# A decoder layer on eight cores: sample caches loaded per head, transfers reordered, and norm squares added in pairs on GpSimd

## The chip, the cores and the metric

The kernel runs on the eight cores of one Trainium2 chip. All cores run the same program, each on its own prompt and on four of the 32 sample tokens. The metric is the device time in microseconds (us) of the slowest core. The cores form two dies, cores 0 to 3 and cores 4 to 7.

In some runs the cores of one die, or of both, are granted a lower TensorE clock, and the run is longer by several per cent; such a run is called slow here. Only fast runs are compared with fast runs, and cores of an undisturbed die with each other.

Short names used by the profile: PE is TensorE's matmuls, PEld its weight loads, DVE is VectorE, ACT is ScalarE, POOL is GpSimd, SP is SyncE.

## The reference

One layer, for 2048 prompt tokens and 4 sample tokens per core, width 1024:

```python
x += 0.5 * SwiGLU(RMSNorm(x))                 # FFN1, hidden width 2816
z  = RMSNorm(x) @ w_in                        # one projection for all branches
# A: dilated window attention, 3 groups x 4 heads x 128. A sample token reads
#    128 rows of its own k/v cache per head, and its new k and v
# B: HGRN2 recurrence, 4 heads, state 128x128
# C: attention into 256 memory tokens, 4 heads (a sample token: cached k/v)
x += merge_branches(A, B, C, gates(z)) @ w_o
x += 0.5 * SwiGLU(RMSNorm(x))                 # FFN2
y  = RMSNorm(x)                               # final norm
# also returned: the window caches shifted by one row (here called bulk copies,
# 44 MB a core, from DRAM to DRAM), the memory k/v, the HGRN states
```

## The kernel before

Activations lie transposed, the 1024 features on partitions in 8 chunks of 128. The 2052 token columns are cut into six tiles of 336 to 352 columns, three for each half of the tokens. The order of stages is: the norm at the start, FFN1, the mixer (branches A, B and C), merge and output projection of half 0 (`merge(0)`, `merge_out(0)`), the same for half 1, FFN2 with the final norm.

Every operation is recorded by a helper (so all have line L80 in the profile), and a list scheduler with a simple cost model fixes for each engine one static order in which it issues. In the trace of the kernel before (core 4) GpSimd keeps to that order: it idles 6.57 us for an x tile in front of three weight loads (`wgu`), until 31.18 us, and only then, at 32.73 us, issues the load of `w_mk`, which needs no x and has the seventh of the seven weight buffers free.

```python
def sq(k, c):                            # sum of squares of one chunk, for a norm
    n = FT[k][1]                         # columns of tile k
    b = P.tile(brp)                      # bf16 buffer
    actf(b.t[:, 0:n], xv(k, c), AF.Square, [dx[k][c]], [b.d])        # ScalarE
    if c == 0:
        pss[k] = P.tile(psS)
    p = pss[k]
    # the matmul with a matrix of 1/1024 sums over partitions: 8 for each norm of a tile
    mm(p.t[:, 0:n], ones_n, b.t[:, 0:n], c == 0, c == 7, [b.d, dc], [p.d])

def merge_out(half, done):
    bs = [load_w(w_o[q]..., 2048) for q in range(4)]
    for k in HT[half]:
        for dp in range(8):
            if half:                     # half 1: x comes back from DRAM chunk by chunk
                xr = P.tile(frp)
                P.dma(SP, ... out=xr.t[:, 0:n], in_=xd[k][:, dp * n:(dp + 1) * n] ...)
            # ... 8 matmuls, x = 0.5 * result + x on VectorE ...
            sq(k, dp)
        done(k)

def att_sample():                        # runs at the end of the mixer
    # ...
    for b in range(NS):                  # 4 sample tokens
        bk = load_w(csk[b]..., 1536)     # cached keys of 12 heads
        bv = load_w(csv[b]..., 1536)     # cached values
        # ... two more loads: cached memory keys and values ...
        # 20 one-column score matmuls, Exp on ScalarE, 20 one-column value
        # matmuls, one ones-matmul, a copy by ScalarE
        yield 1

# bulk copies: one every ~30 us through FFN1, mixer, merge and FFN2
P.dma(ACT, ..., pool="bulk", rel=210e3 + q * 1.45e6 / nbulk)

# the start
load_x(0, xt, 4)
# ...
P.dma(ACT, lambda e: e.dma_start(out=vec[:, 0:52], in_=vecs), writes=[dc])
for k in range(3):
    # ... load tile k, sq(k, c) for 8 chunks, then h = x * rstd * g
gate_up(0, wgu[0], hook)   # weights wait for x only from the second load on

# how the mixer's three branches are interleaved when they are recorded
for _ in spread([A(), HG(), chain(*(mem_att(ti) for ti in range(4)))], [210, 92, 22]):
    pass
```

In the profile `wp` are the weight buffers, `br` and `fr` small bf16 and f32 buffers, `cb` holds the ones-matrices, `ps`, `hb` and `nd` are PSUM banks, `XA` and `XB` hold x or, in the mixer, intermediate results, and `hT` is the normalised x.

The softmax here doesn't subtract the row's maximum and nothing guards it: scores larger than these inputs give would overflow.

## Time and profile before

| | before |
|---|---|
| time, three runs | 1920.39, 1923.39, 2134.98 us (the last is slow) |
| profiled run (fast), cores | 1903.4 to 1930.0 us, slowest core 4 |
| mean granted clock | 0.972 to 0.976 on all cores |

The page of the slowest core, its part 1 (busy us, share of the span, instructions) and part 4 (the chain of work that ended last, by engine):

```profile
PE 1783.9 (92%) x12080; PEld 1123.2 (58%) x12143; DVE 712.1 (37%) x1415; ACT 735.9 (38%) x1227; POOL 296.7 (15%) x437
...
PE 81%; DMA 8%; DVE 3%; issue 3%; ACT 2%; SPq 1%; POOL 1%; DVEq 0%; ACTq 0%; POOLq 0%
```

TensorE is the limit, and 8% of the chain is DMA. Where TensorE is not busy is seen by stage. These are windows of core 4; the columns are the window, its length, each engine's busy us with its instructions, the granted clock, the busy share of the DMA engines, and GB/s:

```profile
0.00:100.00 100.00, 66.17 (x381) 39.23 (x382) 26.27 (x60) 46.49 (x77) 10.69 (x26) 0.95 0.66 128
100.00:517.00 417.00, 416.93 (x2870) 279.96 (x2870) 106.75 (x212) 130.56 (x217) 37.33 (x71) 1.00 0.60 112
527.00:1060.00 533.00, 478.08 (x3108) 257.16 (x3166) 291.50 (x582) 294.70 (x480) 123.90 (x142) 0.97 0.62 135
1060.00:1120.00 60.00, 31.67 (x300) 17.66 (x301) 19.35 (x23) 22.54 (x35) 10.92 (x19) 0.72 0.95 183
1404.00:1453.00 49.00, 32.77 (x210) 20.08 (x210) 18.56 (x38) 15.61 (x28) 2.11 (x4) 0.90 0.84 167
1460.00:1900.00 440.00, 439.98 (x3033) 295.82 (x3031) 103.06 (x203) 107.59 (x185) 36.41 (x69) 1.00 0.55 100
```

FFN1 (100 to 517 us) and FFN2 (1460 to 1900) are full. The start loses 34 us, the mixer (527 to 1060) 55 (42 to 48 on the cores whose trace is complete: core 4's lacks 58 matmul records here, 3108 against 3166 weight loads), its end (1060 to 1120) 28 of 60 us at a clock of 0.72 and a DMA share of 0.95, and the second `merge_out` (1404 to 1453) 16 us on this core.

The timeline of PE on core 4 shows the waits themselves: start and duration in us, the instruction group, and in brackets the idle time before it with what ended it.

```profile
21.32 4.85 PE L80 MATMUL ps<-hT,wp 128*128 128x352 bf16 x16 [2.16 <-DVE hT L80]
...
54.95 0.72 PE L80 MATMUL ps<-hT,wp 128*128 128x336 bf16 x2 [8.75 <-DVE hT L80]
55.46 0.76 PE L80 MATMUL nd<-hT,wp 128*128 128x336 bf16 x2
56.02 0.76 PE L80 MATMUL ps<-hT,wp 128*128 128x336 bf16 x2
...
57.70 0.35 PE L80 MATMUL nd<-hT,wp 128*128 128x336 bf16 x1
...
58.18 0.45 PE L80 MATMUL nd<-hT,wp 128*128 128x336 bf16 x2
58.46 0.45 PE L80 MATMUL ps<-hT,wp 128*128 128x336 bf16 x2
...
1083.73 0.46 PE L80 MATMUL hb<-br,wp 128*128 128x1 bf16 x12 [4.44 <-ACT br L80]
...
1092.52 0.35 PE L80 MATMUL ps<-mqs,wp 128*128 128x1 bf16 x8 [4.96 <-DMA wp<-cmk]
1093.38 0.46 PE L80 MATMUL hb<-br,wp 128*128 128x1 bf16 x12 [0.52 <-ACT br L80]
1100.11 2.29 PE L80 MATMUL ps<-hT,wp 128*128 128x512 bf16 x5 [6.26 <-DMA wp<-w_mq]
...
1112.59 2.50 PE L80 MATMUL ps<-hT,wp 128*128 128x352 bf16 x8 [2.88 <-DMA wp<-w_gb]
```

The projections of FFN1 begin at 21.32 us, and the third x tile is ready only at 54.95. At the mixer's end the one-column matmuls (`128x1`) are the sample's: PE waits 4.44 us for their Exp on ScalarE, 4.96 us for a cached memory key (`cmk`), and then for the weights queued behind the caches (`w_mq`, `w_gb`).

One DMA issue of the first 60 us (KB, and us from issue to landing) shows that the queues are crowded at the start; `memt`, 1024 KB, is in flight then and takes 14.2 us:

```profile
vec<-vecs ACTq DMA_DIRECT2D x1, 26.0 KB, 10.5
```

`vecs`, 26 KB that the first norm needs, takes 10.5 us to land. And this is what PE waited for in the second `merge_out` of core 4 (us in total, times, longest):

```profile
PE hb L80 <- ACT br L80: 16.8, 9, 3.4
```

The ones-matmuls (`hb`) there wait for squares, which wait for x, which waits for the 24 chunk loads.

### The profile page before, as it was taken

The page shows a single profiled execution, that of the slowest core. Times are in us where ns is not written, and L with a number is a line of the kernel's source. Part 1 is how long each engine was busy: PE and PEld are TensorE (multiplying, and loading weights), DVE is VectorE, ACT ScalarE, POOL GpSimd, SP SyncE. Part 2 cuts the span into 40 slices and gives each one's busy share as a digit, 9 for nine tenths or more (in the row PEclk, how much of TensorE's full clock was granted, in tenths as well). Part 3 has the DMA queues.
Part 4 walks back from the last instruction along what each step waited for, and adds up shares of the span by engine and source line. Part 5 has one row for each costly group of instructions (what it writes and reads, how often), then busy time and mean ns, then how long its engine had stood idle before and what let it go on. Part 6 is the DMA issues. An engine that isn't in the chain of part 4 may idle for free.

```text
span 1930.0 us, 32870 instructions; the slowest of 8 cores (1903.4 to 1930.0 us)
## 1 busy us (share of the span) xinstructions
PE 1783.9 (92%) x12080; PEld 1123.2 (58%) x12143; DVE 712.1 (37%) x1415; ACT 735.9 (38%) x1227; POOL 296.7 (15%) x437
## 2 busy tenths in 40 slices
PE   4899999999998998889889489999979999999997
PEld 1566666666644544454445256666645666666665
DVE  2313323221332437675756333463342221332213
ACT  4435324221253646676725343353333221232212
POOL 1010000000131421314001222212200000100010
PEclk9999999999999999999989699999998999999999
DMA  9394449445799864545534986756784654584443
GB/s 190 66 202 74 72 115 159 82 74 109 138 188 167 207 135 100 122 99 124 129 99 111 192 142 110 129 102 96 127 176 89 121 107 81 128 177 76 60 67 104
DMA packets 92699, 233.96 MB, mean 121 GB/s; under 512 B 33280, under 2 KB 43776, under 8 KB 90112
## 3 DMA queue, kind: packets, MB, share of 16 engines
q0 software_dynamic: 40320, 125.98, 42.9%
q1 hardware_dynamic: 50400, 61.73, 10.3%
q10 hardware_dynamic: 1824, 44.15, 8.6%
q8 instruction: 101, 1.65, 0.4%
q14 instruction: 54, 0.44, 0.1%
HBM read 321.27 MB, written 80.51 MB: 208 GB/s over the span
## 4 chain that ended last, share of the span: by engine, by line
PE 81%; DMA 8%; DVE 3%; issue 3%; ACT 2%; SPq 1%; POOL 1%; DVEq 0%; ACTq 0%; POOLq 0%
PE ps L80 46%; PE nd L80 27%; PE hb L80 8%; DMA vd<-br 2%; DMA wp<-cmv 2%; DMA fr<-xd 2%; SPq L80 1%; ACT br L80 1%; DVE XB L80 1%; DMA wp<-w_mq 1%; DMA wp<-cmk 1%; DMA pv<-fr 1%; ACT fr L80 1%; DVE br L80 1%; DVE fr L80 1%
## 5 line engine op out<-in xcount | busy, mean ns | idle before, releaser
L80 PE MATMUL ps<-hT,wp 128*128 128x336 bf16 (+4 forms) x4198 | 699.7, 313 | 31.0 <-DVE hT L80 14.3
L80 PEld LDWEIGHTS ps<-hT,wp 128*128 128x128 bf16 x4232 | 394.2, 98 | 263.7 <-issue 39.5
L80 PE MATMUL nd<-hT,wp 128*128 128x336 bf16 (+2 forms) x2160 | 352.6, 310 | 0.0
L80 ACT ACTIVATE fr<-ps,vec 128x336 f32<-128x336 f32 (+3 forms) x270 | 150.5, 558 | 341.7 <-PE ps L80 339.2
L80 PEld LDWEIGHTS nd<-hT,wp 128*128 128x128 bf16 x2160 | 211.7, 98 | 103.1
L80 PE MATMUL ps<-actb,wp 128*128 128x336 bf16 (+2 forms) x1620 | 260.2, 309 | 0.0
L80 PEld LDWEIGHTS ps<-actb,wp 128*128 128x128 bf16 x1620 | 158.4, 98 | 76.7
L80 ACT ACTIVATE fr<-nd,vec 128x352 f32<-128x352 f32 (+3 forms) x181 | 101.0, 558 | 233.4 <-PE nd L80 233.0
L80 DVE TENSOR_TENSOR actb<-ps,fr 128x336 bf16<-128x336 f32 (+2 forms) x159 | 81.5, 514 | 283.2 <-PE ps L80 244.4
L80 PE MATMUL nd<-actb,wp 128*128 128x336 bf16 (+2 forms) x1068 | 173.3, 308 | 0.0
L80 PEld LDWEIGHTS nd<-actb,wp 128*128 128x128 bf16 x1068 | 104.2, 98 | 50.5
L80 POOL TENSOR_TENSOR fr<-fr 128x512 f32<-128x512 f32 (+3 forms) x96 | 104.2, 1092 | 175.4 <-DVE fr L80 145.9
L80 POOL DMA_DIRECT2D wp<-wgu x88 | 46.7, 530 | 506.4 <-PE ps L80 268.7
L80 DVE TENSOR_TENSOR actb<-nd,fr 128x336 bf16<-128x336 f32 (+2 forms) x105 | 53.8, 513 | 183.3 <-PE nd L80 168.6
L80 ACT ACTIVATE br<-XB,vec 128x352 bf16<-128x352 f32 (+3 forms) x104 | 56.3, 569 | 164.1 <-DVE XB L80 161.7
L80 PE MATMUL hb<-hT,wp 128*128 128x512 bf16 (+1 forms) x543 | 111.4, 342 | 2.8 <-DMA wp<-w_hqf 1.2
L80 ACT ACTIVATE br<-XA,vec 128x336 bf16<-128x336 f32 (+1 forms) x96 | 52.2, 574 | 141.9 <-DVE XA L80 141.6
L80 PE MATMUL hb<-br,cb 128*128 128x336 bf16 (+3 forms) x199 | 60.7, 322 | 39.0 <-ACT br L80 38.6
L80 POOL DMA_DIRECT2D wp<-wd x64 | 33.8, 528 | 357.5 <-PE ps L80 202.7
L80 ACT ACT_TABLE_LOAD x51 | 65.4, 1283 | 39.5 <-PE ps L80 15.4
L80 ACT ACTIVATE fr<-fr,vec 128x512 f32<-128x512 f32 (+3 forms) x105 | 73.4, 702 | 8.9 <-DMA pv<-fr 3.1
L80 DVE SCALAR_TENSOR_TENSOR fr<-fr,ps 128x336 f32<-128x336 f32 (+2 forms) x87 | 44.4, 511 | 87.1 <-ACT fr L80 78.9
(176 smaller groups left out, 1576.3 us busy)
## 6 DMA issues: line engine op xcount, KB each, us to landing
wp<-wgu POOLq DMA_DIRECT2D x88, 512.0 KB, 7.1
wp<-wd POOLq DMA_DIRECT2D x64, 352.0 KB, 4.9
wp<-w_gb POOLq DMA_DIRECT2D x48, 384.0 KB, 8.3
wp<-w_hqf POOLq DMA_DIRECT2D x16, 512.0 KB, 8.2
vd<-br SPq DMA_DIRECT2D x48, 128.0 KB, 9.3
XA<-vd SPq DMA_DIRECT2D x12, 512.0 KB, 6.2
wp<-w_qk POOLq DMA_DIRECT2D x12, 512.0 KB, 7.5
pv<-fr SPq DMA_DIRECT2D x21, 256.0 KB, 6.1
```

The lines of the kernel that those rows point to most:

```text
L80: return f(*[g(x) for x in a], **{n: g(x) for n, x in k.items()})
```

## The change

The intent: take work off TensorE where it is full, and take away what it waits for elsewhere. Five parts:

1. **Pairs.** The squares of two chunks are written in f32, added on GpSimd, and one ones-matmul takes the sum: 4 instead of 8 for each norm of a tile, except in the first three tiles. The scheduler is told to place that matmul 1 us later (`late`).
2. **Samples.** The caches are laid out by head. Each head's cached keys and values (256 KB as bf16) are loaded beside that head's projection, and each memory head's beside its memory attention, so the loads are spread over the mixer.
3. **x.** The second `merge_out` reads x from three whole-tile loads issued before `merge(1)`.
4. **Bulk.** The bulk copies leave the mixer and the second `merge_out`.
5. **Start.** `memt`, the first weight and the constants wait for x; ScalarE's Ln table (a load of 1.28 us in the trace) is loaded early.

```diff
-    def sq(k, c):
+    def sq(k, c, late=1000.0, pair=True):
...
+        if not pair:
+            actf(b.t[:, 0:n], xv(k, c), AF.Square, [dx[k][c]], [b.d])
+            mm(p.t[:, 0:n], ones_n, b.t[:, 0:n], c == 0, c == 7, [b.d, dc], [p.d], late=late)
+        elif c % 2 == 0:
+            pss[k, 0] = P.tile(frp)
+            s = pss[k, 0]
+            actf(s.t[:, 0:n], xv(k, c), AF.Square, [dx[k][c]], [s.d])
+        else:
+            s, s2 = pss[k, 0], P.tile(frp)
+            actf(s2.t[:, 0:n], xv(k, c), AF.Square, [dx[k][c]], [s2.d])
+            tt(POOL, b.t[:, 0:n], s.t[:, 0:n], s2.t[:, 0:n], ALU.add, [s.d, s2.d], [b.d])
+            mm(p.t[:, 0:n], ones_n, b.t[:, 0:n], c == 1, c == 7, [b.d, dc], [p.d], late=late)
...
-            b = load_w(w[j]..., 2048, dx[min(j, 3) - 1] if hook and j else ())
+            b = load_w(w[j]..., 2048, dx[min(j, 3) - 1] if hook and j else dx[0][0:2] if hook else ())
...
-        P.dma(SP, lambda e: e.dma_start(out=memT, in_=memt), writes=d_memT)
+        P.dma(SP, lambda e: e.dma_start(out=memT, in_=memt), reads=dx[2], writes=d_memT)
...
+    def att_s(s, g):                     # called at the end of a head's projection
+        i = g * 4 + s
+        b = load_w(cs[g, s], 1024)       # this head's cached keys and values, 4 tokens
+        ...                              # 4 score matmuls, Exp, 4 value matmuls, 1 of ones
+    def mem_s(h):                        # called at the end of mem_att
+        b = load_w(cm[h], 2048)
+        ...
     def att_sample():
-        for b in range(NS):
-            bk = load_w(csk[b]..., 1536)
-            ...                          # the whole bunched path goes
...
-                if half:
-                    xr = P.tile(frp)
-                    P.dma(SP, ... in_=xd[k][:, dp * n:(dp + 1) * n] ...)
+                xi = x3[:, dp * n:(dp + 1) * n] if k == 3 else xv(k, dp)
...
+    def bulk_at(f):
+        for lo, hi in ((200e3, 480e3), (1130e3, 1340e3), (1440e3, 1760e3)):
+            ...
-        P.dma(ACT, ..., pool="bulk", rel=210e3 + q * 1.45e6 / nbulk)
+        P.dma(ACT, ..., pool="bulk", rel=bulk_at(q / nbulk))
...
-    for _ in spread([A(), HG(), chain(...)], [210, 92, 22]):
+    for _ in spread([A(), HG(), chain(...)], [212, 92, 23]):
         pass
+    att_sample()
...
+    P.dma(SP, lambda e: e.dma_start(out=x3, in_=xd[3]), ...)     # before merge(1)
+    for k in (4, 5):
+        P.dma(SP, ... out=xv(k, 0, 8), in_=xd[k] ...)
     merge(1)
```

## The prediction

> **What bounds the kernel now.** TensorE. On the page of the slowest core (core 4, 1930.0 us) PE is busy 1783.9 us (92%); the chain of waits puts 81% of the span on PE. In windows over FFN1 (100-517 us), merge of half 0 (1120-1400) and FFN2 (1460-1900) PE is busy over 99% at a granted clock of 1.00: only fewer matmuls help there. PE idles in four places (windows of all cores):
> - start, 0-100 us: 34 us idle on every core;
> - mixer, 517-1060: about 45 us, mostly after ACT and DVE;
> - mixer's end, 1060-1120: 24-30 us on every core, DMA share 0.95-1.04, clock about 0.72;
> - second merge_out, 1400-1460: 2.5-7 us on seven cores, 16.8 on core 4.
>
> **What the change does.**
> 1. Halved norms. 168 squares (hook 24, FFN1 48, merge_out 48, FFN2 48) are added in pairs, so 84 ones-matmuls go. In the timeline PE moves on 0.144 us after a 336-column ones-matmul: 84 x 0.144 = 12.1 us, nearly all in PE-bound stages. Cost: 84 GpSimd adds. An f32 add of 128x336 takes GpSimd 0.90 us here (DVE ops of that size 0.51[...]). That is an estimated 76 us on an engine busy 297, hidden because the schedule puts the ones-matmul 1 us later. Only the last norm shows it: +1 us.
> 2. Sample caches. Their loads were bunched at 1064-1100; w_mq and w_gb queued behind them, and PE waited 6.3 us for w_mq, 5.0 for cmk, 2.9 for w_gb. Now each head's share is loaded beside its projection, over about 550 us of mixer. Small matmuls grow from 164 to 180, about 0.025 us each: nothing. The 24-30 us idle should fall to 6-10: -20 us.
> 3. The second merge_out takes x from three whole-tile loads made before merge(1), not 24 chunk loads while it runs: -3 to -5 us on most cores, about -15 on the slowest.
> 4. Bulk copies (44 MB) leave the mixer and merge_out for FFN1, merge and FFN2, at DMA share about 0.6. One copy per 17 us instead of 30: weights should still come in time. The mixer's first part (DMA share 0.9-0.97) gets room: -2 us.
> 5. Start. vecs landed at 12.5 us because memt (1 MB), wgu and cstf shared the queues with x; the first Square waited for it. Memory squares and three table loads then delayed the third tile (PE waited 8.8 us, until 55). These loads now wait for x, and the Ln table (1.28 us in the trace) loads early. -9 us.
>
> Sum: -45 to -48 us on a typical core, the slowest a few more. Predicted, for the slowest core: 1923 - 51 = **1872 us**, 8 in 10 between **1850 and 1895**. Faster by over 2%: **0.77**; within 2%: **0.21**; slower: **0.02**.
>
> **What would show it.** Ones-matmuls (hb<-br,cb and others) fall by 84; PE busy down 10-15 us; start idle about 25; mixer's end idle below 10 at DMA share under 0.9; second merge_out idle under 2 on all cores; dense stages still above 99%; GpSimd busy about 370 us.
>
> **What would make it wrong.** (a) The mixer's end is a chain (last attention block, Ln/Exp, memory attention), not DMA: half of the 20 us stays. (b) The mixer's static order changes throughout; its 88% PE busy at 700-1000 may move 10 us either way. (c) Sample loads take weight slots from w_hqf/w_qk. (d) GpSimd adds delay weight issues in its in-order queue, or denser bulk copies starve weights: gaps in dense stages.

## The result, and the profile after

| | before | after |
|---|---|---|
| time, all runs | 1920.39, 1923.39, 2134.98, 1919.90 us | 1848.73, 2017.46, 1849.07, 1850.35 us |
| median | 1921.89 us | 1849.71 us |
| ratio of the fast runs | 1 | 0.9626 (95%: 0.9604 to 0.9648) |
| cores of the profiled run | 1903.4 to 1930.0 us | 1838.9 to 1847.1 us |

A ratio, here and below, is the mean time of one kernel's fast runs over the mean of the other kernel's fast runs of the same rounds, so it is not quite the ratio of the medians. Each kernel has one slow run (2134.98 and 2017.46 us). The kernel is 3.7% faster, about 72 us, where 51 us was predicted. The median is 0.3 us below the range given; 0.9626 of the 1923.39 us from which the prediction started is 1851.4 us, inside it.

Parts 1, 4 and a line of part 5 of the page after (slowest core, 1847.1 us). The last line is the pair addition: count, then busy us and mean ns, then idle time before with its cause.

```profile
PE 1767.3 (96%) x12075; PEld 1113.0 (60%) x12075; DVE 720.3 (39%) x1439; ACT 733.9 (40%) x1234; POOL 373.6 (20%) x522
...
PE 88%; DVE 4%; ACT 3%; issue 2%; DMA 2%; POOL 0%; DVEq 0%; ACTq 0%; SPq 0%; POOLq 0%
...
L80 POOL TENSOR_TENSOR br<-fr 128x336 bf16<-128x336 f32 (+2 forms) x84 | 76.5, 916 | 160.5 <-ACT fr L80 160.2
```

DMA's share of the chain went from 8% to 2%. GpSimd rose by 76.9 us, which is the 84 additions at 0.916 us. The windows of core 4 that answer to those of before:

```profile
0.00:100.00 100.00, 74.36 (x445) 45.56 (x446) 27.83 (x62) 49.42 (x83) 12.60 (x31) 0.90 0.72 142
100.00:510.00 410.00, 409.95 (x2820) 275.17 (x2820) 107.91 (x212) 125.43 (x212) 69.58 (x105) 1.00 0.64 129
513.00:990.00 477.00, 442.36 (x2960) 240.44 (x3016) 268.66 (x564) 272.43 (x455) 124.58 (x147) 0.96 0.54 117
990.00:1050.00 60.00, 59.19 (x453) 33.84 (x459) 42.63 (x70) 34.60 (x59) 11.37 (x17) 1.00 0.63 118
1348.00:1378.00 30.00, 29.71 (x207) 19.91 (x205) 20.29 (x38) 16.25 (x29) 12.22 (x15) 1.00 0.57 119
1380.00:1830.00 450.00, 450.00 (x3105) 303.11 (x3104) 109.13 (x215) 112.83 (x194) 56.71 (x91) 1.00 0.65 124
```

The start idles 26 us instead of 34. The mixer's end is busy 59 of 60 us with a DMA share of 0.63; the second `merge_out` takes 30 us, all busy. FFN1 and FFN2 stay full though the copies now run there (GpSimd, which issues the weight loads, nearly doubled in FFN1, 37 to 70 us).

The start on core 4, from the timeline of PE, and the landing of `vecs` (`memt` is now issued at 31 us and takes 6.6):

```profile
14.88 4.63 PE L80 MATMUL ps<-hT,wp 128*128 128x352 bf16 x16 [2.17 <-DVE hT L80]
...
45.04 0.72 PE L80 MATMUL ps<-hT,wp 128*128 128x336 bf16 x2 [6.49 <-DVE hT L80]
```

```profile
vec<-vecs ACTq DMA_DIRECT2D x1, 26.0 KB, 5.3
```

`vecs` lands 5 us sooner, the first projection starts 6.4 us sooner and the third tile 10 us sooner. What is left of waits at the mixer's end (core 4, 990 to 1066 us), all of PE's:

```profile
PE nd L80 <- DVE XB L80: 6.2, 2, 4.1
PE ps L80 <- ACT fr L80: 0.2, 1, 0.2
```

No transfer is among them. Those in the second `merge_out`:

```profile
PE ps L80 <- DVE XB L80: 0.3, 1, 0.3
```

**Where the 72 us came from, by stage.** From the trace of PE on every core I took six marks: the first projection matmul, the first matmul of the mixer, the first ones-matmul of `merge_out(0)`, the first and last ones-matmul of `merge_out(1)`, and the end of PE's last matmul. The table has medians of the eight cores in us. "Mixer" runs to the first ones-matmul of `merge_out(0)`, so it contains `merge(0)`. The change shifts that mark 3.3 us later: 42 matmuls of `merge_out(0)` instead of 20 stand before its first ones-matmul, because a pair needs one chunk more (2.2 us, seen against `no_pair`) and because of `late`.

| kernel | start | FFN1 | mixer, merge(0) | of it PE idle | merge_out(0), merge(1) | merge_out(1) | FFN2 |
|---|---|---|---|---|---|---|---|
| before | 21.4 | 506.3 | 716.2 | 72.2 | 157.2 | 36.8 | 466.3 |
| after | 14.8 | 497.1 | 677.7 | 39.0 | 157.0 | 30.5 | 460.0 |
| difference | -6.6 | -9.2 | -38.5 | -33.2 | -0.2 | -6.3 | -6.3 |

Over half of the gain is in the mixer, which was predicted to give 22. Its shortening of 38.5 us is more than the idle time removed, 33.2, though the stage now contains 16 more small matmuls and, through the shifted mark, 22 more of `merge_out(0)`. The rest is clock: on core 7 the mixer went from 717.3 us with PE busy 643.2 at a granted clock of 0.95 (the line is shown under `before_bulk`) to

```profile
513.10:1189.80 676.70, 637.40 (x4373) 360.48 (x4371) 368.77 (x745) 363.62 (x604) 171.70 (x212) 0.97 0.56 119
```

In the traces' records of the granted clock, the mixer has 70 us at half clock before and 39 after (medians of the cores), beside 72.2 and 39.0 us of idle time.

The next table splits the mixer's waits of PE by what ended them (sums of the view of waits over the mixer stage, median of the cores in us). It includes kernels of the experiments below and carries much of the argument.

| kernel | on DMA | on ACT | on DVE | on POOL |
|---|---|---|---|---|
| before | 19.4 | 18.1 | 25.9 | 5.9 |
| before, bulk moved (`before_bulk`, die 1) | 7.0 | 17.6 | 26.0 | 6.0 |
| before, samples and bulk moved (`before_sample_bulk`) | 3.0 | 7.2 | 17.4 | 1.9 |
| after | 4.2 | 7.0 | 23.4 | 2.1 |
| after, bulk put back (`bulk_old`) | 10.5 | 7.2 | 25.0 | 2.0 |
| after, samples put back (`sample_old`) | 7.8 | 18.4 | 27.2 | 5.9 |
| after, other listing order (`order`) | 3.8 | 14.2 | 28.4 | 1.2 |

### The profile page after: what moved, and what is told of

It reads as the page before. It is cut to its first block, busy times and chain, and to the rows that moved or that the text cites. A ratio compares the mean times of both kernels' runs of the same rounds, so it can differ in the third digit from the quotient of the medians.

```text
span 1847.1 us, 33000 instructions; the slowest of 8 cores (1838.9 to 1847.1 us)
## 1 busy us (share of the span) xinstructions
PE 1767.3 (96%) x12075; PEld 1113.0 (60%) x12075; DVE 720.3 (39%) x1439; ACT 733.9 (40%) x1234; POOL 373.6 (20%) x522
## 4 chain that ended last, share of the span: by engine, by line
PE 88%; DVE 4%; ACT 3%; issue 2%; DMA 2%; POOL 0%; DVEq 0%; ACTq 0%; SPq 0%; POOLq 0%
PE ps L80 51%; PE nd L80 28%; PE hb L80 9%; DVE XB L80 1%; ACT fr L80 1%; DMA XA<-xt 1%; DMA wp<-w_mq 1%; DVE fr L80 1%; ACT br L80 1%; DVE br L80 1%; ACT L80 1%; DVE hT L80 1%; DVE actb L80 0%; DVE XA L80 0%; POOL fr L80 0%
## 5 line engine op out<-in xcount | busy, mean ns | idle before, releaser
L80 PEld LDWEIGHTS ps<-hT,wp 128*128 128x128 bf16 x4216 | 389.7, 98 | 242.5 <-issue 25.7
L80 ACT ACTIVATE fr<-nd,vec 128x336 f32<-128x336 f32 (+3 forms) x176 | 98.3, 559 | 223.4 <-PE nd L80 223.1
L80 PE MATMUL nd<-actb,wp 128*128 128x336 bf16 (+2 forms) x1046 | 166.2, 308 | 0.5 <-ACT fr L80 0.5
L80 PE MATMUL hb<-hT,wp 128*128 128x512 bf16 (+1 forms) x592 | 126.1, 348 | 0.0
L80 POOL TENSOR_TENSOR br<-fr 128x336 bf16<-128x336 f32 (+2 forms) x84 | 76.5, 916 | 160.5 <-ACT fr L80 160.2
L80 ACT ACTIVATE fr<-XB,vec 128x352 f32<-128x352 f32 (+2 forms) x96 | 53.3, 578 | 138.3 <-DVE XB L80 138.0
L80 ACT ACTIVATE fr<-XA,vec 128x336 f32<-128x336 f32 (+1 forms) x72 | 40.9, 578 | 129.9 <-DVE XA L80 129.9
L80 PEld LDWEIGHTS hb<-hT,wp 128*128 128x128 bf16 x592 | 50.2, 100 | 50.0 <-issue 4.1
```

What stands on the lines that cost most here:

```text
L80: return f(*[g(x) for x in a], **{n: g(x) for n, x in k.items()})
```

## The experiments

The question was why the mixer gave twice what was expected. The theory from the prediction: the sample's bunched loads at its end. The first rival: the new static order of the mixer is simply a lucky one. The second: moving the bulk copies out of the mixer is worth much more than the 2 us predicted. The other parts were each undone once to measure their sizes. Every run gave the right result. Each had five rounds. The kernel before had slow runs of its own on each of the three chips of the experiments, and on two of them nearly slow ones, which widens the intervals there; stages are then read from the profiles, of which there is one for each kernel.

A kernel "before, with the samples spread, nothing else" could not be built: the scheduler's buffer pools locked. Two more listing orders locked as well.

### Samples put back: `sample_old`

The changed kernel with the old bunched sample path and the old listing weights.

```diff
-        att_s(s, g)                      # in the head's projection
-        mem_s(ti)                        # in the memory attention
+                smp = att_sample()       # old: four batches beside the last block
+                    next(smp, None)
-... [212, 92, 23]
+... [210, 92, 22]
```

> The changed kernel with the old sample-attention path (all cache loads bunched at the end of the mixer), everything else as changed. Theory S (the sample caches alone make the mixer's end): the idle time of PE around the end of the mixer returns from 7-8 us to 25-30 us and the run costs +20 us over the changed kernel (ratio to before about 0.973); the body of the mixer keeps its idle time of about 30 us. Rival O (spread sample work and the changed issue order also filled the body): the body goes back to 40-45 us as well and the cost is +30 us or more (ratio 0.978 or above). Rival D (DMA room from the moved bulk copies would have cured the end by itself): end idle stays under 15 us and the cost is under 8 us.

Measured: 1878.62 us, ratio to before 0.9781 (0.9763 to 0.9799), so about 30 us slower than the changed kernel. The mixer took 704.5 us instead of 677.7. PE idle in the last 180 us before `merge_out(0)` was 17 to 20 us against 7 to 8 in the changed kernel and 25 to 29 before. In the earlier part it was 42.9 us, against 31.4 in the changed kernel and 45.2 before.

The wait at the sample's own matmuls is back to the hundredth (timeline of PE, core 4):

```profile
1059.52 0.46 PE L80 MATMUL ps<-br,wp 128*128 128x1 bf16 x12 [4.44 <-ACT br L80]
```

What follows: the sample's bunching cost the end about 11 us with the bulk copies out of the way, not 20, and more by waits on ScalarE than by late transfers. The end's 20 us was shared with the bulk copies (`before_bulk` below: moving them alone takes 7 us off the end). But undoing this part also costs the earlier mixer 12 us, so it can't be read apart from the static order, which it changes throughout. That is what the first rival says; it needed its own test.

### Only another listing order: `order`

```diff
-    for _ in spread([A(), HG(), chain(...)], [212, 92, 23]):
+    for _ in spread([A(), HG(), chain(...)], [212, 92, 24]):
```

> The changed kernel with one weight of the interleave changed (memory attention 23 to 24), which moves only the order in which the mixer's work is listed. If the mixer's idle time is a matter of a lucky static order (rival O), the time from the mixer's start to the first ones-matmul of merge_out moves by more than 5 us and the ratio by more than 0.003. If the order matters little, both stay: ratio 0.961 to 0.9645, mixer idle 37-41 us in all.

Measured: 1865.18 us, ratio 0.9706 (0.9687 to 0.9726). The mixer took 690.0 us, 12 more than the changed kernel, with the same work and the same transfers. In the table of waits DMA stays (3.8 against 4.2), ACT rises by 7 and DVE by 5. So the order alone moved this mixer by 12 us, as the prediction had feared under (b). One other order was run, so this is one sample of the effect; a difference of that size between two mixers that differ in order need not have another reason.

### Bulk put back: `bulk_old`

```diff
-        P.dma(ACT, ..., pool="bulk", rel=bulk_at(q / nbulk))
+        P.dma(ACT, ..., pool="bulk", rel=210e3 + q * 1.45e6 / nbulk)
```

> The changed kernel with the bulk copies spread evenly over 210-1660 us again. Theory B (the mixer's body gained its unpredicted 11-25 us because the bulk copies left it): body idle goes from 30 back to 40 us or more, the slowest core loses more than the median core, +10 us or more (ratio to before 0.968 or above). Rival O (issue order and spread sample work did it): body idle stays at 28-33 us and the time stays within 3 us of the changed kernel (ratio 0.961 to 0.9645).

Measured: 1860.03 us, ratio 0.9685 (0.9666 to 0.9704), 11 us slower than the changed kernel. The mixer took 685.8 us, idle 46.8. The timeline of PE on core 4 has the reason:

```profile
523.97 3.42 PE L80 MATMUL ps<-hT,wp 128*128 128x512 bf16 x8 [10.70 <-DMA wp<-w_hqf]
```

and the waits of core 1 in the mixer:

```profile
PE hb L80 <- DMA wp<-w_v: 9.5, 1, 9.5
```

A weight that comes 10 us late is enough: DMA waits rose by 6.3 us, the others by at most 1.6. PE's static order can't be the reason: PE runs the first 1282 matmuls of the mixer in the same order in both kernels, and there they took 220.0 us instead of 212.5 (medians of the cores), while the rest of the mixer took 464.1 instead of 465.1. (Two profiles of one order differ by 3.3 us in `hg_late` below.) This theory held; the 2 us of the prediction was too small.

### Bulk moved in the kernel before: `before_bulk`

The same test from the other end: the kernel before with `bulk_at`, nothing else.

```diff
-        P.dma(ACT, ..., pool="bulk", rel=210e3 + q * 1.45e6 / nbulk)
+        P.dma(ACT, ..., pool="bulk", rel=bulk_at(q / nbulk))
```

> The kernel before with only the bulk copies moved to the three windows of the change. Theory B: the body of the mixer loses 10 us of idle time on a typical core and about 20 on the slowest, time -10 to -20 us (ratio 0.990 to 0.995); the second merge_out also loses some of its 5-17 us, because a bulk copy no longer runs beside its loads. Rival O: body idle stays at 40-45 us on typical cores and the ratio is 0.996 or above.

Measured: fast runs 1896.46, 1893.04 and 1894.37 us, ratio 0.9862 (0.9840 to 0.9884), 26 us faster. (The median of all six runs, 1940.03 us, has three slow ones in it.) The profiled run was slow on die 0, so only die 1 is read: the mixer 690.6 to 698.2 us against 716.2.

The mixer of core 7 in the kernel before, as one window:

```profile
526.90:1244.20 717.30, 643.22 (x4334) 359.90 (x4332) 363.78 (x714) 357.69 (x589) 170.62 (x210) 0.95 0.69 138
```

and in this one:

```profile
526.80:1225.00 698.20, 640.40 (x4334) 360.38 (x4332) 363.70 (x714) 358.32 (x589) 170.37 (x210) 0.96 0.58 115
```

The DMA share fell from 0.69 to 0.58. PE runs the same 4334 matmuls in 2.8 us less busy time: that is the clock, since no work was taken away. In the table of waits DMA falls by 12.4 us, and ACT, DVE and POOL stay within 0.5. Moving the copies also shifts the static order of the later mixer, and most of the gain lies there (14 us, against 3 in the first 330 us, where the order is nearly the same); since waits on other engines didn't move, I read the gain as the transfers', but no run here holds the order fixed. It is more than the 10 to 20 us expected, and lies elsewhere: idle time in the earlier part fell by 5 us, not 10 (45.2 to 40.6), and in the last 180 us by 7 (26.1 to 18.9); the second `merge_out` fell from 36.8 to 33.5. That the gain is larger than in the changed kernel (26 against 11 us) fits with these two: there the copies cost nothing at the end (7.7 us idle in `bulk_old` too) nor in the second `merge_out` (30.5 in both).

### Samples and bulk together in the kernel before: `before_sample_bulk`

```diff
+        att_s(s, g)
+        mem_s(ti)
-    ... att_sample() beside the last block, [210, 92, 22]
+    ... att_sample() after the mixer, [212, 92, 23]
-    rel=210e3 + q * 1.45e6 / nbulk
+    rel=bulk_at(q / nbulk)
```

> The kernel before with two parts of the change, the spread sample caches and the moved bulk copies. From mixer start to the first ones-matmul of merge_out the kernel before takes 709-719 us, with moved bulk copies 691-698, the changed kernel 673-679. Theory S (sample caches and bulk copies together are the whole gain of the mixer): 673-682 us here, ratio about 0.975 to 0.978. Rival (part of the mixer's gain comes from the particular static order of the changed kernel): 683 us or more, ratio 0.980 or above.

Measured: 1870.02 us (fast runs 1864.63 to 1872.99), ratio 0.9721 (0.9663 to 0.9778). The mixer took 662.4 us, idle 31.8: better than the changed kernel's 677.7, of which 3.3 is the shift of the mark. So these two parts give all of the mixer's gain and more. The first rival falls as far as it said that the changed kernel has a lucky order: this one has a better; the 12 us between them are no more than an order can make. Compared with `before_bulk`, the samples took 10 us of ACT waits, 9 of DVE, 4 of POOL and 4 of DMA. The second `merge_out` took 40.7 us here, 7 more than in `before_bulk`, which is not explained.

### Pairing undone: `no_pair`

```diff
-    def sq(k, c, late=1000.0, pair=True):
+    def sq(k, c, late=1000.0, pair=False):
```

> The changed kernel with every square again multiplied by ones on its own (84 ones-matmuls more, no GpSimd adds). Theory P (PE-bound, each ones-matmul worth 0.144 us): 12.1 us more in the dense stages, less up to 3 us that pairing costs where a norm ends a stage (mixer start, last norm): +9 to +12 us, ratio to before 0.967 to 0.969; the spacing from mixer start to first merge_out stays within 3 us. Rival Q (the paired sums cost waits elsewhere, so that the gain was mostly eaten): under +5 us.

Measured: 1858.50 us (fast runs 1856.27 to 1858.75), ratio 0.9668 (0.9602 to 0.9734). FFN1 took 502.3 us instead of 497.1: 36 ones-matmuls more there (12 of the hook's second-half tiles, 24 of FFN1) at 0.144 us make 5.2, exactly. From the first ones-matmul of `merge_out(0)` to the end of FFN2 it took 652.1 us instead of 647.5: 48 more make 6.9, and the end waits 2.3 us less (below); the shift of the mark blurs this sum by up to 2.2. The mixer was 5 us shorter, 2.2 of it the mark. The count of `hb<-br,cb` matmuls on a core is 209 here and 125 in the changed kernel: 84. (In all, a complete core has 12143 matmuls before and 12075 after, 68 fewer: 84 gone and 16 small ones more.)

At the end of the kernel nothing follows the last norm, and pairing shows. The last ones-matmul of the changed kernel, core 4, timeline:

```profile
1836.91 0.90 POOL L80 TENSOR_TENSOR br<-fr 128x340 bf16<-128x340 f32 x1 [6.66 <-ACT fr L80]
1837.96 0.30 PE L80 MATMUL hb<-br,cb 128*128 128x340 bf16 x1 [3.41 <-POOL br L80]
```

and of this one:

```profile
1837.12 0.30 PE L80 MATMUL hb<-br,cb 128*128 128x340 bf16 x1 [0.88 <-ACT br L80]
```

PE waits 3.41 us for square, addition and signals; without pairing 0.88, and 0.26 for one more ones-matmul after it. So pairing is worth about 8 us by the times and 9.8 by these two stretches, and the prediction's 11 was near.

### x loads put back: `x_old`

```diff
-                xi = x3[:, dp * n:(dp + 1) * n] if k == 3 else xv(k, dp)
+                if half:
+                    xr = P.tile(frp)
+                    P.dma(SP, ... in_=xd[k][:, dp * n:(dp + 1) * n] ...)
...
-    P.dma(SP, lambda e: e.dma_start(out=x3, in_=xd[3]), ...)     # and the loads of tiles 4 and 5
```

> The changed kernel with the 24 chunk loads of x inside the second merge_out again. Theory X1 (chunk loads alone cost it): the second merge_out stretches from 30.5 us to 35 us on a typical core, ratio 0.965 or above. Theory X2 (most of the 5 to 19 us was lost to the bulk copies and weight loads running beside the chunk loads; with the bulk copies moved the chunk loads cost 2 to 4 us, as the kernel before with moved bulk copies showed 32 to 34.5 us): ratio 0.963 to 0.965.

Measured: 1862.48 us, ratio 0.9692 (0.9648 to 0.9736), 13 us slower. The second `merge_out` took 51.9 us against 30.5, more than in the kernel before (36.8): none of the sizes expected came out. The mixer was by chance 10 us shorter (667.6), some 3 of it in the part whose order is the same as in the changed kernel, so the 13 us hides some 21. The waits of core 4 in the second `merge_out`:

```profile
PE ps L80 <- DVE XB L80: 6.3, 2, 3.4
PE nd L80 <- DVE XB L80: 4.6, 2, 3.0
PE hb L80 <- POOL br L80: 3.3, 2, 1.8
```

PE idles 12.9 us in this stage (median of the cores; 0.3 in the changed kernel); the rest of the 21 us goes with a clock that is at half for 13.7 us of the stage. Either pairing takes two more `fr` buffers, for which the chunk loads compete, or the chunk loads meet other traffic.

### x loads put back and pairing undone: `x_old_no_pair`

Both diffs above together.

> The changed kernel with chunk loads in the second merge_out and without pairing. With chunk loads and pairing that merge_out took 51.9 us, with whole-tile loads 30.5, in the kernel before with moved bulk copies 33.3, and with spread samples too 40.7. Theory F (the pair sums hold buffers of the pool that the chunk loads are read into, so the loads come later): 33 to 42 us here. Rival C (a bulk copy that now falls into merge_out slows the loads, pairing has no part in it): 48 us or more.

Measured: 1863.08 us, ratio 0.9670 (0.9617 to 0.9723). The second `merge_out` took 46.5 us. Pairing thus accounts for 5.4 of the 21 us, and neither of the two expected numbers was hit. The copies were the other suspect. In both kernels each core issues one bulk copy inside this `merge_out`, and in `before_bulk` (33.5 us) none. But the kernel before has one there on every core too and took 36.8 us, and `before_sample_bulk` issues none there (one about 5 us ahead) and took 40.7. Nor do the landing times order the kernels: the first tile's 176 KB chunk loads took a median of 8 to 9.5 us in `before_bulk`, 14 in the kernel before, 12 to 14 in `before_sample_bulk`, 10 to 12 in `x_old` and 19 in `x_old_no_pair` (cores 4 and 5). No run moved the copy alone. So most of the 21 us stays open. What is shown is that with whole-tile loads made early this `merge_out` took 30.5 to 30.8 us on every core, in every kernel that has them and pairs.

### The start put back: `start_old`

```diff
-            b = load_w(..., dx[min(j, 3) - 1] if hook and j else dx[0][0:2] if hook else ())   # first weight
+            b = load_w(..., dx[min(j, 3) - 1] if hook and j else ())
-        P.dma(SP, ... in_=memt), reads=dx[2], writes=d_memT)
+        P.dma(SP, ... in_=memt), writes=d_memT)
-    P.op(ACT, ... func=AF.Ln ...)        # early table load
-        elif j == 8:                     # constants
+        if j == 2:                       # constants, beside mem_load
-        elif j in (9, 11, 13):
+        elif j in (8, 10, 12):
```

> The changed kernel with the old start: memory rows, float constants and first weights loaded at once beside x, no early Ln. Expected from the traces: first projection matmul at 21 us instead of 14.8, third tile at 55 instead of 45, mixer start 10 us later, and all of it kept to the end: +9 to +11 us, ratio 0.967 to 0.969. If the static order of later stages shifts with it, the spacing from mixer start to first merge_out moves by more than 3 us; then the start's share is read from the mixer start alone.

Measured: 1860.83 us, ratio 0.9685 (0.9636 to 0.9733), 11 us slower. The first projection came at 21.3 us again, the mixer began 9.5 us later, and it took what it took in the changed kernel (677.1). This part was sized nearly right (9). Its steps were undone together, so what each is worth was not measured.

### The HGRN sample's matmuls later: `hg_late`

The changed kernel has one 5.0 us wait of PE at the sample step of HGRN, where a matmul stands in the static order before its operand is ready.

```diff
-  mm(op_.t[:, col:col + 1], s0.t[...], sg[:, col:col + 1], True, True, [...], [op_.d])
+  mm(op_.t[:, col:col + 1], s0.t[...], sg[:, col:col + 1], True, True, [...], [op_.d], late=6000.0)
```

> The changed kernel, with the scheduler told to list the small float matmuls of the HGRN sample step 6 us later; PE's order is the same up to that step. In the changed kernel PE stands 5.0 us before them, waiting for DVE, and the granted clock falls to 0.75 there. Theory order (the mixer's length in the changed kernel, 673-679 us, contains a local wait that its static order makes): that wait falls under 2 us and the mixer shortens by 4 to 10 us, ratio to before 0.957 to 0.961. Rival (the wait is made up elsewhere): mixer within 2 us of 677.7, ratio 0.961 to 0.9645.

Measured: 1846.87 us (1842.40 to 1850.08), ratio 0.9583 (0.9524 to 0.9643). On every core PE's longest wait for VectorE's `fr` in the mixer is 3.8 us, against 5.0 in the changed kernel; whether the 3.8 stand before the same matmul is not on record. The mixer took 672.5 us, 5 less than in the changed kernel. But 3.3 of the 5 lie in the first 2749 matmuls, whose order is the same in both kernels (425.1 and 421.8 us, medians of the cores), so most of it is not the edit's: single profiles of one order differ by that much. The interval contains the changed kernel's 0.9626, so it is not shown to be faster.

### Four squares for one ones-matmul: `quad`

```diff
+            if c % 4 == 1:
+                pss[k, 1] = b
+            else:                        # add the two pair sums, too, on GpSimd
+                tt(POOL, b.t[:, 0:n], b0.t[:, 0:n], b.t[:, 0:n], ALU.add, [b0.d, b.d], [b.d])
-            mm(...)                      # for every pair
+                mm(...)                  # for every four
```

> The changed kernel with pairs of pairs: GpSimd adds two pair sums, so two ones-matmuls per norm instead of four. If a ones-matmul is worth 0.144 us of PE-bound time, 42 fewer give 6 us, of which about 1.5 us is lost at the last norm and at the mixer's start: -3 to -5 us apart from shifts of the mixer's static order; the projection stage before the mixer shortens by 2.6 us. Rival (GpSimd's in-order queue begins to delay weight issues): PE idle appears in dense stages and the time rises.

Measured: 1851.96 us (fast runs 1850.42 to 1852.60), ratio 0.9610 (0.9543 to 0.9678): no gain, though 42 more ones-matmuls went. FFN1 became 1.0 us shorter, where 18 fewer ones-matmuls would make 2.6. By the marks the mixer is 3.5 us longer and `merge_out(1)` 3.2 shorter (30.5 to 27.3), but that is the marks' own shift: 65 matmuls of `merge_out(0)` now stand before its first ones-matmul instead of 42, some 3.4 us. From the first matmul of `merge_out(0)` to PE's end it took 2.2 us longer, though 24 ones-matmuls fewer should save 3.5. PE's waits ate that: they rose from 1.3 to 2.9 us in `merge_out(0)` and `merge(1)`, from 0.3 to 1.1 in `merge_out(1)` and from 3.4 to 6.7 in FFN2. The end of core 4 shows the largest:

```profile
1831.82 0.90 POOL L80 TENSOR_TENSOR br<-fr 128x340 bf16<-128x340 f32 x1 [7.84 <-ACT fr L80]
1832.86 0.83 POOL L80 TENSOR_TENSOR br<-br 128x340 bf16<-128x340 bf16 x1
1833.84 0.44 PE L80 MATMUL hb<-br,cb 128*128 128x340 bf16 x1 [6.36 <-POOL br L80]
```

A second addition lengthens the last wait from 3.4 to 6.4 us. The addition with bf16 inputs (0.83 us) is hardly cheaper than that with f32 inputs (0.90 in the same timeline), with as many elements and half the bytes read; why is not shown.

### Both: `quad_late`

The two diffs above together, as a candidate for a version better than both kernels.

> Pairs of pairs and the later HGRN sample matmuls together, a candidate that may beat the changed kernel. If the two gains add: 1849.7 - 4 - 6 = about 1840 us, ratio 0.955 to 0.960. If the mixer's static order moves against it, 0.962 or above.

Measured: 1848.31 us (fast runs 1846.23 to 1850.36), ratio 0.9591 (0.9532 to 0.9650). Again the interval contains the changed kernel. No version clearly beats it; `hg_late` has the lowest time seen, 1842.40 us.

## Why the prediction was right, and where its sizes were off

The class and the mechanism were right: each part that was said to save time does, and the signs that were listed came, one of them (PE's busy time) larger than listed. The sum was some 30% too small, and the result lies at the very edge of the range; that it lies no further out is in part luck, since three of the terms (samples, x, bulk) were too small by about 9 us each.

- Ones-matmuls fell by 84 (209 to 125 between `no_pair` and the changed kernel). PE busy fell by 21.7 us, from 1789.2 to 1767.5 (medians of the six cores whose traces are complete; core 4's 1783.9 lacks 63 matmul records), 10 to 15 predicted: the rest goes with the clock, see 3.
- The start idles 26 us (25 predicted).
- The mixer's end (the last 180 us before `merge_out(0)`) idles 7 to 8 us on all cores (6 to 10 predicted), at a DMA share of 0.63 (core 4, 990 to 1050 us).
- The second `merge_out` idles 0.3 us (under 2 predicted), FFN1 and FFN2 stay full, GpSimd is busy 373.6 us (370 predicted).

The sum was 51 us and the gain 72. The sizes of the terms, undone one at a time from the changed kernel; a difference of ratios times the 1921 us of before, so each has an uncertainty of about 5 to 13 us:

| part | predicted | ratio when undone, less 0.9626 | us |
|---|---|---|---|
| pairs | 11 | 0.0042 | 8 |
| samples | 20 | 0.0155 | 30 |
| x | 3 to 5, slowest core 15 | 0.0066 | 13 |
| bulk | 2 | 0.0059 | 11 |
| start | 9 | 0.0059 | 11 |
| sum | 45 to 48, slowest a few more | | 73 |

That the sum comes so near to the total gain is partly chance, since the parts overlap: from the kernel before, bulk alone gave 26 us.

1. **The bulk term failed: "The mixer's first part (DMA share 0.9-0.97) gets room: -2 us."** I had read that PE waited little for DMA in the mixer's first part, and stopped there. The copies cost in two other ways. With the copies there, PE waited some 10 us for one weight (10.70 us for `w_hqf`, 9.5 for `w_v` in `bulk_old`), and they took part in the jam at the mixer's end: moving them alone took 7 of its 26 us of idle time. The term measures 11 us in the changed kernel and 26 in the one before.
2. **The sample term was credited with the whole end and nothing else: "The 24-30 us idle should fall to 6-10: -20 us."** The end fell as said, but the samples' share of it is about 11 us (`sample_old`); the copies have the rest, and only while the samples are bunched (`bulk_old` idles 7.7 us there). And spreading them eased the earlier mixer too: without them ACT waits of the whole mixer fall from 18 to 7 us. How much of that is the spread itself and how much a different static order is not settled; `order` moved ACT and DVE waits by 12 us without touching the samples.
3. **No term stood for the clock.** After the 8.75 us gap at the start PE ran at half speed for 2.75 us, and for longer where gaps followed each other (27 us at the mixer's end), and with the idle time busy time fell too: 2.8 us for the same 4334 matmuls in `before_bulk`, 5.8 us on core 7 from before to after, there with 38 matmuls more in the stage.
4. **The x term was sized from the kernel before** (3 to 5 us on most cores). In the changed kernel the chunk loads would have cost 21 us in that stage: 5.4 through pairing, the rest open. A saving measured in the old surroundings wasn't the saving in the new.
5. Pairs and start were sized nearly right. Of the reservations, (a) holds for the 6 us still left at the end (a wait on VectorE in the memory attention), (b) was real (12 us in `order`), and (c) and (d) did not come.

## What to carry to other kernels

Price a gap of TensorE in a mixed stage at more than its length, because here 16.3 us less idle time in the mixer came with 2.8 us less busy time for the same matmuls (`before_bulk`), and look at what shares the queues with a late transfer, not only at the transfer that is named as the releaser: here the background copies belonged where TensorE is full and weights are loaded well ahead (moving them there gave 11 us in the changed kernel and 26 in the one before). Sort waits by releaser for a whole stage (DMA, ACT, DVE) before and after; that told the copies' share from the samples' where the times alone couldn't. With a static order fixed by a scheduler, change nothing but the order once, to learn how large a difference can mean nothing; here it was 12 us of 690. Where two kernels share the order of a first part, compare that part: in `bulk_old` it alone settled that the loss was not the order's.

## What else the traces show

- The granted clock. In the fast state each of the eight cores ran dense matmuls for 450 us (1380 to 1830 us after the change, PE busy 447 us or more) at a granted clock of 1.00; but every core's time counts from its own start, and nothing in the traces shows when the cores ran beside each other. In the slow run of `before_bulk` the four cores of die 0 had a mean clock of 0.93, those of die 1 0.98. On die 0 the clock was 0.81 for 508 us: on core 0 in FFN2 and on core 2 in FFN1. What sets it is not shown. Core 0, FFN1 and FFN2:

```profile
61.00:569.00 508.00, 504.26 (x3401) 330.94 (x3399) 137.73 (x271) 171.05 (x280) 55.96 (x97) 1.00 0.74 128
1465.00:1973.00 508.00, 504.80 (x2878) 312.66 (x2876) 101.57 (x201) 103.77 (x178) 33.34 (x63) 0.81 0.56 107
```

  and core 2 of the same run:

```profile
61.00:569.00 508.00, 507.91 (x2900) 315.38 (x2900) 109.42 (x218) 139.79 (x229) 39.77 (x76) 0.81 0.60 104
1465.00:1973.00 508.00, 503.62 (x3471) 338.30 (x3468) 137.55 (x274) 138.92 (x237) 41.50 (x78) 1.00 0.67 127
```

- The clock after gaps. In a mixed stage with gaps of many lengths it came to 2.8 us of busy time beside 16.3 us less idle (`before_bulk` against before, core 7, the windows above).
- Transfers. In the page of before the loads of a weight of 512 KB (1 MB in DRAM, in f32) took a median of 7.1 to 8.2 us from issue to landing, and 176 KB chunk loads 8 to 19 us in the second `merge_out`, of the kernels compared under `x_old_no_pair`. What a background copy costs one of them was not measured.
- The issue order alone: 12 us of a 690 us stage (`order`).
